# Expert weights stored with an expert's tiles side by side in each row, and loaded two tiles at a time

## The chip, the cores and the metric

The kernel runs on one core of a Trainium2 chip. The metric is the time of one execution on the device, in microseconds (us).

## The reference

The reference runs two transformer blocks over 256 tokens of width 1024, in float32. The first has a mixing sublayer (stick-breaking attention and gated linear attention) and a convolutional FFN. The second has a pooling and attention sublayer and a mixture of 32 experts, of which each token takes 4. Only the experts matter here:

```python
def expert_block(args):
    xblk, e = args
    gu = xblk @ w_gate_up[e] + b_gate_up[e]           # w_gate_up[e]: 1024 x 2048
    gate = jnp.minimum(gu[:, :D_EXPERT], SWIGLU_LIMIT)
    up = jnp.clip(gu[:, D_EXPERT:], -SWIGLU_LIMIT, SWIGLU_LIMIT)
    act = gate * jax.nn.sigmoid(SWIGLU_ALPHA * gate) * (up + 1)
    return act @ w_down[e] + b_down[e]                # w_down[e]: 1024 x 1024
```

Each expert brings 12.6 million bytes of weights that are used once, so the 32 experts read 403 MB from DRAM.

## The kernel before

The first block, the second block's attention and the router come first; then the experts run in order, 0 to 31 (the expert with the most tokens is exchanged with number 16 on the way, so SP reads from a table on the chip which expert's weights to load).

An expert's weights are six tiles of 128 partitions by 4096 floats (16 KB in each partition, 2048 KB in all, called 2 MB below): tiles 0 and 1 hold the gate matrix, 2 and 3 the up matrix, 4 and 5 the down matrix. Here a tile is numbered through all experts: tile 6e + j is tile j of expert e, so tile 100 is the first down tile of expert 16. In DRAM (`wexp`) the array is [32, 6, 128, 4096]: each tile is one contiguous piece.

Tiles go through a ring of 11 slots (`RING`), made of pools `ra`, `rb`, `rx`, `rc`, `re` and `rd`. `ring_tile` takes the next slot; `eload` issues the load on SP's DMA queue. SP runs its loads in program order. A load waits until PE has made its last use of the tile that held the slot before, and each of the 8 semaphores for loads (`DMAHW0` to `DMAHW7`) must have counted its previous load, so at most 8 loads are under way.

PE runs one expert in this order: `hidden` multiplies the gate tiles (32 matmuls into `g`, 16 for each tile), then the up tiles (32 into `u`), both at L1398; `turn` transposes; `down` (L1423) multiplies the two down tiles, 16 for each tile. For expert 16, `over_hidden` and `over_down` run the tokens beyond 64 through the same six tiles once more, so PE keeps these tiles for a second sweep, and the down tiles are used last of all by the ordinary `down`. Experts 30 and 31 are written out by hand at the end, with the last two down tiles loaded in smaller pieces.

```python
def eload(i, t=None, cuts=(0, 4096)):
    if t is None:
        t = ring_tile()
    src = a["wexp"][i // 6, i % 6]
    ...
    for p, q in zip(cuts, cuts[1:]):
        nc.sync.dma_start(out=t[:, p:q], in_=src[:, p:q])
    return t
```

Of the kernel before, what the change touches and what calls it, by code (L numbers as in the profile page):

```python
# [8 lines left out]
F32 = mybir.dt.float32  # L9
# [10 lines left out]
P = 128  # L20
# [4 lines left out]
NE = 32  # L25
# [3 lines left out]
RING_A = 3  # L29
RING_B = 2  # L30
RING_X = 2
RING_C = 4
RING = RING_A + RING_B + RING_X + RING_C
HOT = 16
HOT_FROM = 4
HOT_TO = 30
# [83 lines left out]
def layout(inp):  # L120
    a = {k: np.asarray(v) for k, v in inp.items()}
    o = {}
    o["xT"] = a["x"][0].T.reshape(DC, P, T).transpose(1, 0, 2)
    col = lambda v: np.asarray(v).reshape(-1, P).T
    vec = np.zeros((P, NVEC), np.float32)
    for name, v in (("norm_mix", a["norm_mix_g"]), ("b_gate", a["b_gate"]), ("gla_norm", a["gla_norm_g"]),
                    ("norm_ffn", a["norm_ffn_g"]), ("conv_w", a["conv_w"]), ("conv_b", a["conv_b"]),
                    ("norm_final", a["norm_final_g"]), ("attn_norm", a["g_attn_norm_2"]),
                    ("b_pool", a["b_pool_2"]), ("pool_scale", a["pool_scale_2"]), ("q_a", a["g_q_a_2"]),
                    ("kv_a", a["g_kv_a_2"]), ("out_pool", a["g_out_pool_2"]), ("out_attn", a["g_out_attn_2"])):  # L130
        s, e = VEC[name]
        vec[:, s:e] = col(v)
    o["vecs"] = vec
    o["cst"], o["cst1"], o["cst2"] = constants()
    w = a["w_in"][0]
    kp = lambda m: m.reshape(-1, P, m.shape[-1]).transpose(1, 0, 2)
    o["wga"] = kp(w[:, 3072:3088])
    o["win"] = np.stack([kp(w[:, s:s + 512]) for _, s in W_IN_ORDER])
    o["wau"] = a["w_alpha_up"][0]
    o["bal"] = a["b_alpha"]  # L140
    o["wbr"] = np.stack([kp(a["w_branch_sb"][0]), kp(a["w_branch_gla"][0])])
    o["wout"] = np.stack([kp(a["w_out"][0][:, s:s + 512]) for s in (0, 512)])
    wf = a["w_ffn_in"][0]
    o["wfi"] = np.stack([kp(np.concatenate([wf[:, b:b + 128] for b in
                                            (256 * j, 2816 + 256 * j, 256 * j + 128, 2944 + 256 * j)], 1))
                         for j in range(11)])
    o["wfo"] = kp(a["w_ffn_out"][0])
    w2 = a["w_in_2"][0]
    kr = w2[:, 896:928]
    o["win2"] = np.stack([kp(np.concatenate([w2[:, 512:896]] + [kr, kr[:, 16:], kr[:, :16]] * 2, 1)), kp(w2[:, :512])])  # L150
    wq = a["w_q_b_2"][0].reshape(256, 8, 96)
    o["wq"] = kp(np.concatenate([wq, wq[:, :, 80:96], wq[:, :, 64:80]], 2).reshape(256, 1024))
    wkv = a["w_kv_b_2"][0].reshape(128, 8, 128)
    o["wkv"] = np.concatenate([wkv[:, :, :64].reshape(128, 512), wkv[:, :, 64:].reshape(128, 512)], 1)
    o["wpool"] = a["w_pool_2"][0].transpose(1, 0, 2)
    o["pos"] = a["positions_2"]
    o["wo2"] = kp(a["w_out_2"][0])
    o["gf2"] = np.concatenate([col(a["g_ffn_norm_2"]), col(a["g_final_2"])], 1)
    o["wr"] = kp(a["w_router_2"][0])
    o["br"] = a["b_router_2"]  # L160
    wgu = a["w_gate_up_2"][0].reshape(NE, 2, 4, P, 2, D)
    wdn = a["w_down_2"][0].reshape(NE, 1, 2, 4, P, D)
    o["wexp"] = np.concatenate([wgu.transpose(0, 4, 1, 3, 2, 5).reshape(NE, 4, P, 4096),
                                wdn.transpose(0, 1, 2, 4, 3, 5).reshape(NE, 2, P, 4096)], 1)
    o["wexp"][NE - 1, 4:6] = wdn[NE - 1, 0].reshape(2, 4, P, 2, 512).transpose(3, 2, 0, 1, 4).reshape(2, P, 4096)
    o["bgu"] = np.concatenate([a["b_gate_up_2"][0].reshape(NE, 2, 2, 512).transpose(2, 0, 1, 3).reshape(64, 1024)] * 2, 0)
    o["bdn"] = a["b_down_2"][0]
    return {k: np.ascontiguousarray(v) for k, v in o.items()}


def build(nc, tc, a, out, dump=lambda name, ap: None, upto=99):
# [6 lines left out]
    with ctx:  # L178
        enter = ctx.enter_context
        enter(tc.manual_schedule(engines={PE, mybir.EngineType.SP}))  # L180
        cp = enter(tc.tile_pool(name="cp", bufs=1))
        ring = [enter(tc.tile_pool(name="ra", bufs=RING_A))] * RING_A
        rx = enter(tc.tile_pool(name="rx", bufs=RING_X))
        aux = enter(tc.tile_pool(name="aux", bufs=4, space=PSUM))
        front = ExitStack()
        fenter = front.enter_context
# [31 lines left out]
        who, who_at = {}, []  # L218

        def eload(i, t=None, cuts=(0, 4096)):  # L220
            if t is None:
                t = ring_tile()
            src = a["wexp"][i // 6, i % 6]
            if HOT_FROM <= i // 6 <= HOT_TO:
                if i // 6 not in who:
                    who.clear()
                    who[i // 6] = nc.values_load(who_at[0][0:1, i // 6:i // 6 + 1], engines=[mybir.EngineType.SP],
                                                 min_val=0, max_val=NE - 1)
                src = a["wexp"][bass.ds(who[i // 6], 1), i % 6].rearrange("o p n -> (o p) n")
            for p, q in zip(cuts, cuts[1:]):  # L230
                nc.sync.dma_start(out=t[:, p:q], in_=src[:, p:q])
            return t

        def bank(pool, name):
            return pool.tile([P, 512], F32, name=name)
# [233 lines left out]
        for tt in range(2):  # L469
            o = aps[:, tt * 256:(tt + 1) * 256]  # L470
# [80 lines left out]
        for par in range(2):  # L551
            rows = slice(par * 64, par * 64 + 64)
            for hh in range(2):
                h = 2 * hh + par
                for tt in range(2):
                    o = og[par][:, hh * 256 + tt * 128:hh * 256 + (tt + 1) * 128]
                    mm(o, gv[:, tt, h * 128:(h + 1) * 128], attT[:, par, hh * 2 + tt, :],
                       start=hh == 0 and tt == 0, stop=False, skip_group_check=True)
                for n in range(1, 4):
                    o = og[par][:, hh * 256 + n * 64:hh * 256 + (n + 1) * 64]  # L560
# [204 lines left out]


        ats.close()
        ring.extend([enter(tc.tile_pool(name="rb", side="left", bufs=RING_B))] * RING_B)
        tp = xs.enter_context(tc.tile_pool(name="fp", side="right", bufs=2))
        table("gelu_apprx_tanh_and_others")  # L770
        acc = [bank(aux, "aux") for _ in range(4)]
# [37 lines left out]
        for j in range(11):  # L809
            w = wload(a["wfi"][j].rearrange("p k n -> p (k n)")) if j else wf0  # L810
            if j % 2 == 1 or j == 10:
                k0 = 4 * (j // 2)
                n = min(4, NF - k0)
# [36 lines left out]
        for c2 in range(4):  # L850
            q = tp.tile([P, 2, 2, T], F32, name="nsq", bufs=2)
# [58 lines left out]
        wexp = [eload(i) for i in range(RING - RING_C - 2)]  # L910
# [18 lines left out]
        ra = rb = b3.tile([P, 2, T], F32, name="pt")  # L929
# [140 lines left out]
        prs_done = [False]  # L1070
# [43 lines left out]
        for step, _ in enumerate(hd):  # L1114
            if step == 1:
                next(pm_)
                next(res)
            if step == 3:
                next(res)
            if prs_done[0] and len(wexp) < RING - RING_C - 1:  # L1120
                bx.close()
                ring[:0] = [enter(tc.tile_pool(name="rc", side="left", bufs=1))]
                wexp.append(eload(len(wexp)))
            if step >= 14:
                fill(outp, 1)
        b3x.close()
        ring[:0] = [enter(tc.tile_pool(name="re", side="left", bufs=1))]
        wexp.append(eload(len(wexp)))
        fill(outp, 99)
        wexp.append(eload(len(wexp)))  # L1130
        x2m = bX.tile([P, 2, D], F32, name="X")
# [26 lines left out]
        front.close()  # L1158


        ring[:0] = [enter(tc.tile_pool(name="rd", side="left", bufs=RING_C - 2))] * (RING_C - 2)
        mo = enter(tc.tile_pool(name="mo", side="right", bufs=1))
        rt = ExitStack()
        rp = rt.enter_context(tc.tile_pool(name="rp", side="right", bufs=1))
# [19 lines left out]
        for tt in range(2):  # L1184
            for nh in range(2):
# [4 lines left out]
                o = hT[:, tt, 4 * nh:4 * nh + 4, :].rearrange("p a b -> p (a b)")  # L1190
# [7 lines left out]
        for tt in range(2):  # L1198
            for c in range(DC):
                q = 32 * (c % 4)  # L1200
# [265 lines left out]
        def over_rest(e, wx, room, block):  # L1466
            with over_if(e, block):
                def fetch(j):
                    for i in range(2):
                        nc.scalar.dma_start(out=wx[i], in_=a["wexp"][e, j + i])  # L1470

                fetch(0)
                over_hidden(e, wx, wx, room, block, own=True, between=lambda: fetch(2))
                fetch(4)
                over_down(e, wx, room, block, own=True)
# [15 lines left out]

        LAST = 6 * NE - 8
        for e in range(NE - 2):
            while len(wexp) < 6 * e + 6:
                wexp.append(eload(len(wexp)))
            wg, wu, wd = (wexp[6 * e + 2 * i:6 * e + 2 * i + 2] for i in range(3))
            odd = e % 2
            um = wk.tile([P, 512], F32, name="um")
# [5 lines left out]
                scatter(onehots([0, 1], gcol, "og"), ot)  # L1504
                at = turn(um)
            if odd:
                while len(wexp) < min(6 * e + 4 + RING, LAST):
                    wexp.append(eload(len(wexp)))
            if e and not odd:
                combine(*pend, 0)  # L1510
                at = turn(um)
# [7 lines left out]
            elif odd:  # L1519
# [3 lines left out]
                gather(xg, oh, 2 * CAP, 1)  # L1523
                ot_next = ot_tile()
                scatter(onehots([e + 1, e + 2], gcol, "og"), ot_next)
            while len(wexp) < min(6 * e + 4 + RING, LAST):
                wexp.append(eload(len(wexp)))
            if not odd:
                ds = rooms["ds"]
            ps = down(at, wd)  # L1530
# [9 lines left out]
                           start=False, stop=False, skip_group_check=True)  # L1540
            for dh in range(2):
                nc.scalar.copy(ds[odd * 64:odd * 64 + 64, dh * 512:(dh + 1) * 512], ps[dh * 64:dh * 64 + 64, :])  # L1542
            while len(wexp) < min(6 * e + 6 + RING, LAST):
                wexp.append(eload(len(wexp)))
            if odd:
                pend = (ot, ds)
                ot = ot_next
# [2 lines left out]
        p, q = NE - 2, NE - 1  # L1550
# [58 lines left out]
        wx = [ring_tile() for _ in range(2)]  # L1609
# [24 lines left out]
```

## Time and profile before

| | |
|---|---|
| median of 3 runs | 1415.34 us (1415.24 to 1419.24) |
| the profiled execution's own time | 1415.02 us |
| its span, first to last instruction | 1413.2 us |
| PE busy | 1364.8 us, 97% of the span |
| DVE, ACT, POOL busy | 33%, 25%, 11% of the span |
| loads of expert tiles on SP's queue | 190 of 2 MB and 6 smaller ones |

The span lies 1.8 us under the execution's own time; what lies around it is start and end. Times in the trace count from the start of the span. PE is TensorE, SP the engine that issues the loads; a load "lands" when its semaphore has its full count.

### The profile page before, as it was taken

To read this page: it belongs to the slowest core of one execution; us is meant where nothing else is said; L and a number is where in the kernel's file an instruction comes from. 1 tells how busy PE (TensorE), PEld (TensorE's weight loads), DVE (VectorE), ACT (ScalarE), POOL (GpSimd) and SP (SyncE) were. 2 spreads that over 40 slices of the span, in tenths; PEclk is the share of its full clock that TensorE was granted. 3 is DMA by queue.
4 is the path that set the end of the run, shared out by engine and by line. 5 is a ranking of instruction groups with operands and counts; after the bars stand their busy time and mean duration, and the time that the engine had idled before them with its cause. 6 is when DMAs were issued, how large, how long until landed. Compare 5 with 4: busy or idle time off the path is not lost.

```text
span 1413.2 us, 18906 instructions
## 1 busy us (share of the span) xinstructions
PE 1364.8 (97%) x7842; PEld 791.8 (56%) x7842; DVE 472.9 (33%) x777; ACT 354.7 (25%) x583; POOL 151.6 (11%) x240
## 2 busy tenths in 40 slices
PE   8999999999999999999999999998999999999896
PEld 7999999999997733433333333343334334333333
DVE  5556778676698521101101111110111111111111
ACT  5355755444455510010001001000100100100002
POOL 0001221112120021011011011010101101101010
PEclk9999999999999999999999999999999999999999
DMA  8334257345356789999999999999999999999995
GB/s 301 150 142 155 98 229 289 129 179 209 148 203 258 312 372 429 419 428 428 428 427 428 429 427 427 428 428 427 428 428 427 428 429 426 427 429 427 428 427 219
DMA packets 38866, 482.13 MB, mean 341 GB/s; under 512 B 4289, under 2 KB 8018, under 8 KB 9586
## 3 DMA queue, kind: packets, MB, share of 16 engines
q1 hardware_dynamic: 38722, 480.69, 81.8%
q8 instruction: 64, 1.05, 0.3%
q14 instruction: 32, 0.26, 0.0%
q10 hardware_dynamic: 48, 0.13, 0.0%
HBM read 479.75 MB, written 1.05 MB: 340 GB/s over the span
## 4 chain that ended last, share of the span: by engine, by line
PE 73%; DMA 19%; DVE 4%; ACT 2%; issue 1%; POOL 1%; SPq 0%; ACTq 0%; POOLq 0%
DMA w<-in_wexp 19%; PE tr L1423 12%; PE g L1398 12%; PE u L1398 11%; PE mm L306 6%; PE mm L307 6%; PE mm L309 6%; PE tr L1369 3%; PE aux L1479 3%; PE mm L348 2%; PE aux L1098 1%; PE aux L804 1%; PE aux L803 1%; PE aux L805 1%; DMA w<-in_win 1%; PE u L1393 1%
## 5 line engine op out<-in xcount | busy, mean ns | idle before, releaser
L1398 PE MATMUL u<-w,X 128*64 128x512 f32 x1056 | 235.4, 596 | 6.5 <-DMA w<-in_wexp 6.5
L1398 PE MATMUL g<-w,X 128*64 128x512 f32 x1056 | 234.3, 595 | 1.6 <-DMA w<-in_wexp 0.8
L1423 PE MATMUL tr<-w,sg 128*64 128x512 f32 x992 | 223.1, 603 | 9.1 <-ACT ot L1379 6.9
L1403 DVE TENSOR_SCALAR um<-g 128x512 f32<-128x512 f32 x32 | 22.1, 692 | 503.8 <-PE g L1398 503.8
L1398 PEld LDWEIGHTS u<-w,X 128*64 128x64 f32 x1056 | 72.3, 137 | 148.7 <-issue 135.6
L1423 PEld LDWEIGHTS tr<-w,sg 128*64 128x64 f32 x992 | 69.3, 138 | 149.7 <-issue 136.0
L1398 PEld LDWEIGHTS g<-w,X 128*64 128x64 f32 x1056 | 72.7, 137 | 141.5 <-issue 138.2
L306 PE MATMUL mm<-w,hi 128*128 128x256 f32 x608 | 150.4, 286 | 0.0
L307 PE MATMUL mm<-w,hi 128*128 128x256 f32 x608 | 148.0, 281 | 0.0
L300 DVE TENSOR_TENSOR lo<-w,hi 128x1024 fp32r<-128x1024 f32 x108 | 132.4, 1226 | 36.3 <-ACT hi L299 36.3
L299 ACT ACTIVATE hi<-w 128x1024 fp32r<-128x1024 f32 x108 | 114.0, 1060 | 90.6 <-PE mm L307 72.1
L306 PEld LDWEIGHTS mm<-w,hi 128*128 128x128 f32 x608 | 115.1, 189 | 1.4 <-issue 0.9
L307 PEld LDWEIGHTS mm<-w,hi 128*128 128x128 f32 x608 | 115.3, 190 | 0.4 <-issue 0.2
L1542 ACT COPY X<-tr 64x512 f32<-64x512 f32 x60 | 34.8, 580 | 225.0 <-PE tr L1423 221.3
L309 PE MATMUL mm<-w,lo 128*128 128x256 f32 x608 | 84.6, 281 | 0.0
L1407 DVE TENSOR_SCALAR sg<-u 128x512 f32<-128x512 f32 x33 | 22.8, 691 | 182.1 <-PE u L1398 182.1
L1416 ACT COPY sg<-tr 128x512 f32<-128x512 f32 x33 | 19.4, 587 | 256.0 <-PE tr L1413 256.0
L309 PEld LDWEIGHTS mm<-w,lo 128*128 128x128 f32 x608 | 77.4, 188 | 0.0
L1404 ACT ACTIVATE sg<-um 128x512 f32<-128x512 f32 x32 | 20.2, 630 | 220.7 <-DVE um L1403 220.7
L1383 POOL CAST pick<-selb 128x128 fp32r<-128x128 f32 x32 | 9.3, 293 | 573.3 <-PE u L1393 573.3
L1479 PE MATMUL aux<-X,ot 128*128 128x512 f32 x128 | 61.6, 606 | 0.0
L1369 PE MATMUL tr<-oh,xh 128*128 128x128 f32 (+1 forms) x256 | 51.3, 282 | 4.8 <-DVE X L1372 4.8
(477 smaller groups left out, 1690.5 us busy)
## 6 DMA issues: line engine op xcount, KB each, us to landing
w<-in_wexp SPq DMA_DIRECT2D x190, 2048.0 KB, 29.1
w<-in_win SPq DMA_DIRECT2D x11, 2048.0 KB, 7.4
w<-in_wfi SPq DMA_DIRECT2D x11, 2048.0 KB, 9.0
w<-in_wfo SPq DMA_DIRECT2D x5, 2048.0 KB, 13.3
w<-in_wbr SPq DMA_DIRECT2D x2, 2048.0 KB, 8.7
w<-in_wout SPq DMA_DIRECT2D x2, 2048.0 KB, 7.3
w<-in_wo SPq DMA_DIRECT2D x2, 2048.0 KB, 7.7
w<-in_wexp SPq DMA_DIRECT2D x3, 1024.0 KB, 34.3
```

The lines of the kernel that those rows point to most:

```text
L299: act(hv, src, AF.Copy)
L300: vtt(lv, src, hv.bitcast(F32), op=OP.subtract)
L306: mm(ps, hv[:, k, :], xh[:, k, :], start=start and k == 0, stop=False, skip_group_check=True)
L307: mm(ps, hv[:, k, :], xl[:, k, :], start=False, stop=False, skip_group_check=True)
L309: mm(ps, lv[:, k, :], xh[:, k, :], start=False, stop=k == nk - 1, skip_group_check=True)
L348: mm(ps[tt], lhs, (hv, hv, lv)[part][:, kk, :], start=u == 0 and part == 0 and kk == 0, stop=u == 3 and part == 2 and kk == 1)
L1369: mm(ps[:, j * n:(j + 1) * n], xn[i // 2][:, i % 2, c * 128:(c + 1) * 128], oh[:, i % 2, :], start=i == 0, stop=i == 3)
L1398: mm(gu[i][hf * 64:hf * 64 + 64, :], xg[:, k, :], ws[k // 4][:, (k % 4) * D + hf * 512:(k % 4) * D + (hf + 1) * 512], start=late and k == ...
L1407: vts(t, gu[1], LIMIT, -LIMIT, op0=OP.min, op1=OP.max)
L1423: mm(ps[dh * 64:dh * 64 + 64, :], at[:, k % 4, k // 4, :], wd[k // 4][:, (k % 4) * D + dh * 512:(k % 4) * D + (dh + 1) * 512], start=k == ...
L1479: mm(y[tt][dh], ot[rows, tt * 128:(tt + 1) * 128], ds[rows, dh * 512:(dh + 1) * 512], start=False, stop=False, skip_group_check=True)
L1542: nc.scalar.copy(ds[odd * 64:odd * 64 + 64, dh * 512:(dh + 1) * 512], ps[dh * 64:dh * 64 + 64, :])
```

## The change

In DRAM the six tiles of an expert now lie side by side in each row: `wexp` is [32, 128, 24576], so one partition's part of a tile is 16 KB out of a row of 96 KB, and the parts of tiles j and j+1 follow each other.

The ring keeps its 11 slots, but its parts are now windows of 3 (`ra`), 2 (`rb`), 2 (`rx`), 2 (`rc`, in place of `rc` and `re`) and 2 (`rd`) slots, in which tiles of one or of two slots follow each other and wrap to the start.

From tile 22 on, `eload_to` takes two tiles at once where both are of one expert, where the next two slots are of one part and where at least 8 tiles remain. Such a pair is one 4 MB transfer with runs of 32 KB in each partition, has one semaphore, and its two slots come free together.

```diff
+    o["wexp"] = o["wexp"].transpose(0, 2, 1, 3).reshape(NE, P, 6 * 4096)
...
+        def slots(name, n, **kw):
+            return enter(tc.tile_pool(name=name, bufs=1, side="left", **kw)).ring(n * 4096 * 4, name=name)
+
+        ring = [slots("ra", RING_A)] * RING_A
+        rx = slots("rx", RING_X)
...
             for p, q in zip(cuts, cuts[1:]):
-                nc.sync.dma_start(out=t[:, p:q], in_=src[:, p:q])
+                nc.sync.dma_start(out=t[:, p:q], in_=src[:, o + p:o + q])
             return t
+
+        def eload_to(wexp, limit):
+            while len(wexp) < limit:
+                i = len(wexp)
+                if i >= 2 * RING and i % 6 != 5 and ring[0] is ring[1] and i + 2 <= 6 * NE - 8:
+                    if i + 2 > limit:
+                        break
+                    ring.extend([ring.pop(0), ring.pop(0)])
+                    t = ring[-1].tile([P, 8192], F32, name="w")
+                    eload(i, t, (0, 8192))
+                    wexp += [t[:, 0:4096], t[:, 4096:8192]]
+                else:
+                    wexp.append(eload(i))
...
-            if prs_done[0] and len(wexp) < RING - RING_C - 1:
+            if prs_done[0]:
                 bx.close()
-                ring[:0] = [enter(tc.tile_pool(name="rc", side="left", bufs=1))]
-                wexp.append(eload(len(wexp)))
...
-        ring[:0] = [enter(tc.tile_pool(name="re", side="left", bufs=1))]
-        wexp.append(eload(len(wexp)))
+        ring[:0] = [slots("rc", 2, reuse_waits="tile")] * 2
+        eload_to(wexp, len(wexp) + 2)
...
-            while len(wexp) < min(6 * e + 4 + RING, LAST):
-                wexp.append(eload(len(wexp)))
+            eload_to(wexp, min(6 * e + 4 + RING, LAST))
```

SP's order shows the pairs in two places. The first is the loads after expert 16's: a name `w_n` is one ring tile, 128x4096 is 2 MB and 128x8192 is 4 MB, and the rows between that only set addresses are left out. Before, these are tiles 107 to 113, one load each:

```order
L231 DMA w_7687<-in_wexp 128x4096 [waits DMAHW2_49,PE_49]
L231 DMA w_7689<-in_wexp 128x4096 [waits DMAHW3_49,PE_49]
L231 DMA w_7701<-in_wexp 128x4096 [waits DMAHW4_49,PE_49]
L231 DMA w_7703<-in_wexp 128x4096 [waits DMAHW5_49,PE_49]
L231 DMA w_7724<-in_wexp 128x4096 [waits DMAHW6_49,PE_49]
L231 DMA w_7726<-in_wexp 128x4096 [waits DMAHW7_49,PE_49]
L231 DMA w_7779<-in_wexp 128x4096 [waits DMAHW0_49,PE_49]
```

After the change the rows of the same place hold the pairs (104, 105), (106, 107), (108, 109), (110, 111) and (112, 113), and the single tile 114:

```order
L236 DMA w_7435<-in_wexp 128x8192 [waits DMAHW0_49,PE_49]
L236 DMA w_7621<-in_wexp 128x8192 [waits DMAHW2_49,DMAHW1_49,PE_49]
L236 DMA w_7623<-in_wexp 128x8192 [waits DMAHW3_49,PE_49]
L236 DMA w_7654<-in_wexp 128x8192 [waits DMAHW4_49,PE_49]
L236 DMA w_7707<-in_wexp 128x8192 [waits DMAHW6_49,DMAHW5_49,PE_49]
L236 DMA w_7709<-in_wexp 128x4096
```

Tile 110 had a load and a wait of its own, and now waits with tile 111. The pair (110, 111) takes the two slots of the pair (99, 100); the pair (112, 113) takes the slot of tile 101 and one of the pair (102, 103).

The second place is the last tiles that pairs can take. Before, these are the loads of tiles 179 to 184:

```order
L231 DMA w_9145<-in_wexp 128x4096 [waits DMAHW2_49,PE_49]
L231 DMA w_9147<-in_wexp 128x4096 [waits DMAHW3_49,PE_49]
L231 DMA w_9159<-in_wexp 128x4096 [waits DMAHW4_49,PE_49]
L231 DMA w_9161<-in_wexp 128x4096 [waits DMAHW5_49,PE_49]
L231 DMA w_9182<-in_wexp 128x4096 [waits DMAHW6_49,PE_49]
L231 DMA w_9307<-in_wexp 128x4096 [waits DMAHW7_49,PE_49]
```

After the change the rows are the pair (178, 179), tile 180, the pair (181, 182), tile 183 and tile 184:

```order
L236 DMA w_9021<-in_wexp 128x8192 [waits DMAHW6_49,DMAHW5_49,PE_49]
L236 DMA w_9023<-in_wexp 128x4096
L236 DMA w_9035<-in_wexp 128x8192 [waits DMAHW7_49,PE_49]
L236 DMA w_9056<-in_wexp 128x4096 [waits DMAHW0_49,PE_49]
L236 DMA w_9181<-in_wexp 128x4096
```

The last pair joins expert 30's second gate tile (181) to its first up tile (182); what follows is loaded singly, as before. Over the whole of SP's order 64 loads are 128x8192, 31 of them up to the pair (99, 100) and 35 up to (108, 109). Up to tile 21 the rows are those of before, and the rows of PE are the same throughout.

## Rows read from the trace of the kernel before

**Rows 1.** The page: span, and DMA share and rate in 40 slices of 35.3 us.
```profile
span 1413.2 us, 18906 instructions
...
DMA  8334257345356789999999999999999999999995
...
GB/s 301 150 142 155 98 229 289 129 179 209 148 203 258 312 372 429 419 428 428 428 427 428 429 427 427 428 428 427 428 428 427 428 429 426 427 429 427 428 427 219
```

**Rows 2.** Busy time by engine in one stretch of two experts (53.4 us).
```profile
core 0: us, PE busy (x) PEld busy (x) DVE busy (x) ACT busy (x) POOL busy (x), PEclk, DMA share, GB/s
...
1046.89:1100.29 53.40, 52.62 (x247) 20.07 (x247) 6.92 (x10) 5.14 (x10) 4.50 (x10) 1.00 1.01 428
```

**Rows 3.** PE's waits for expert tiles, whole span: us in total, times, longest.
```profile
PE u L1398 <- DMA w<-in_wexp: 6.5, 9, 1.2
...
PE g L1398 <- DMA w<-in_wexp: 0.8, 1, 0.8
...
PE tr L1432 <- DMA w<-in_wexp: 0.4, 1, 0.4
```

**Rows 4.** PE in order of time, experts 15 and 16: start, length, instruction, [idle before].
```profile
914.42 3.65 PE L1398 MATMUL u<-w,X 128*64 128x512 f32 x16 [0.30 <-DMA w<-in_wexp]
...
938.89 3.65 PE L1398 MATMUL u<-w,X 128*64 128x512 f32 x16 [0.43 <-DMA w<-in_wexp]
...
943.79 3.65 PE L1398 MATMUL u<-w,X 128*64 128x512 f32 x16 [1.25 <-DMA w<-in_wexp]
...
986.05 7.09 PE L1423 MATMUL tr<-w,sg 128*64 128x512 f32 x32 [0.73 <-ACT sg L1416]
```

**Rows 5.** PE in order of time, experts 30 and 31 (same columns).
```profile
1345.14 7.09 PE L1398 MATMUL g<-w,X 128*64 128x512 f32 x32
...
1353.07 3.65 PE L1398 MATMUL u<-w,X 128*64 128x512 f32 x16 [0.41 <-DMA w<-in_wexp]
...
1357.97 3.65 PE L1398 MATMUL u<-w,X 128*64 128x512 f32 x16 [1.25 <-DMA w<-in_wexp]
...
1377.56 3.65 PE L1398 MATMUL u<-w,X 128*64 128x512 f32 x16 [0.59 <-DMA w<-in_wexp]
...
1394.87 3.46 PE L1432 MATMUL tr<-w,sg 128*64 128x256 f32 x30 [0.40 <-DMA w<-in_wexp]
```

**Rows 6.** SP's issues of tiles 100, 110, 111, 114 and 182: start, length.
```profile
909.60 0.33 SPq L231 DMA_DIRECT2D w<-in_wexp  x1
...
970.36 0.33 SPq L231 DMA_DIRECT2D w<-in_wexp  x1
...
989.75 0.33 SPq L231 DMA_DIRECT2D w<-in_wexp  x1
...
1000.63 0.33 SPq L231 DMA_DIRECT2D w<-in_wexp  x1
...
1314.17 0.34 SPq L231 DMA_DIRECT2D w<-in_wexp  x1
```

**Rows 7.** Issue to landing, us, of tiles 8, 100, 110 and 182.
```profile
w<-in_wexp SPq DMA_DIRECT2D x1, 2048.0 KB, 7.6
...
w<-in_wexp SPq DMA_DIRECT2D x1, 2048.0 KB, 39.0
...
w<-in_wexp SPq DMA_DIRECT2D x1, 2048.0 KB, 28.8
...
w<-in_wexp SPq DMA_DIRECT2D x1, 2048.0 KB, 38.9
```

**Rows 8.** SP's queue at 620 to 730 and 417 to 418.2 us: packets, MB, share.
```profile
q1 hardware_dynamic: 3222, 46.91, 100.3%
...
q1 hardware_dynamic: 233, 0.47, 100.7%
```

**Rows 9.** A w_ffn_out tile issued at 322.18; all engines' window while it moves.
```profile
w<-in_wfo SPq DMA_DIRECT2D x1, 2048.0 KB, 13.5
...
331.20:335.20 4.00, 4.00 (x36) 4.00 (x35) 2.92 (x5) 1.23 (x2) 0.86 (x1) 1.00 1.01 434
```

More of the change, by code (lines that the diff above doesn't have):

```diff
@@ L181, in build @@
         cp = enter(tc.tile_pool(name="cp", bufs=1))
-        ring = [enter(tc.tile_pool(name="ra", bufs=RING_A))] * RING_A
-        rx = enter(tc.tile_pool(name="rx", bufs=RING_X))
+        def slots(name, n, **kw):
+            return enter(tc.tile_pool(name=name, bufs=1, side="left", **kw)).ring(n * 4096 * 4, name=name)
+        ring = [slots("ra", RING_A)] * RING_A
+        rx = slots("rx", RING_X)
         aux = enter(tc.tile_pool(name="aux", bufs=4, space=PSUM))
@@ L220, in eload @@
         def eload(i, t=None, cuts=(0, 4096)):
+            e, o = i // 6, i % 6 * 4096
             if t is None:
                 t = ring_tile()
-            src = a["wexp"][i // 6, i % 6]
-            if HOT_FROM <= i // 6 <= HOT_TO:
-                if i // 6 not in who:
+            src = a["wexp"][e]
+            if HOT_FROM <= e <= HOT_TO:
+                if e not in who:
                     who.clear()
-                    who[i // 6] = nc.values_load(who_at[0][0:1, i // 6:i // 6 + 1], engines=[mybir.EngineType.SP],
-                                                 min_val=0, max_val=NE - 1)
-                src = a["wexp"][bass.ds(who[i // 6], 1), i % 6].rearrange("o p n -> (o p) n")
+                    who[e] = nc.values_load(who_at[0][0:1, e:e + 1], engines=[mybir.EngineType.SP],
+                                            min_val=0, max_val=NE - 1)
+                src = a["wexp"][bass.ds(who[e], 1)].rearrange("o p n -> (o p) n")
             for p, q in zip(cuts, cuts[1:]):
-                nc.sync.dma_start(out=t[:, p:q], in_=src[:, p:q])
+                nc.sync.dma_start(out=t[:, p:q], in_=src[:, o + p:o + q])
             return t
+        def eload_to(wexp, limit):
[10 more added lines that the diff above has]
+                    wexp.append(eload(i))
         def bank(pool, name):
@@ L767, in build @@
         ats.close()
-        ring.extend([enter(tc.tile_pool(name="rb", side="left", bufs=RING_B))] * RING_B)
+        ring.extend([slots("rb", RING_B)] * RING_B)
         tp = xs.enter_context(tc.tile_pool(name="fp", side="right", bufs=2))
@@ L1158, in build @@
         front.close()
-        ring[:0] = [enter(tc.tile_pool(name="rd", side="left", bufs=RING_C - 2))] * (RING_C - 2)
+        ring[:0] = [slots("rd", RING_C - 2, reuse_waits="tile")] * (RING_C - 2)
         mo = enter(tc.tile_pool(name="mo", side="right", bufs=1))
@@ L1469, in fetch @@
                     for i in range(2):
-                        nc.scalar.dma_start(out=wx[i], in_=a["wexp"][e, j + i])
+                        nc.scalar.dma_start(out=wx[i], in_=a["wexp"][e, :, (j + i) * 4096:(j + i + 1) * 4096])
                 fetch(0)
@@ L1493, in build @@
         for e in range(NE - 2):
-            while len(wexp) < 6 * e + 6:
-                wexp.append(eload(len(wexp)))
+            eload_to(wexp, 6 * e + 6)
             wg, wu, wd = (wexp[6 * e + 2 * i:6 * e + 2 * i + 2] for i in range(3))
@@ L1506, in build @@
             if odd:
-                while len(wexp) < min(6 * e + 4 + RING, LAST):
-                    wexp.append(eload(len(wexp)))
+                eload_to(wexp, min(6 * e + 4 + RING, LAST))
             if e and not odd:
@@ L1525, in build @@
                 scatter(onehots([e + 1, e + 2], gcol, "og"), ot_next)
-            while len(wexp) < min(6 * e + 4 + RING, LAST):
-                wexp.append(eload(len(wexp)))
+            eload_to(wexp, min(6 * e + 4 + RING, LAST))
             if not odd:
@@ L1542, in build @@
                 nc.scalar.copy(ds[odd * 64:odd * 64 + 64, dh * 512:(dh + 1) * 512], ps[dh * 64:dh * 64 + 64, :])
-            while len(wexp) < min(6 * e + 6 + RING, LAST):
-                wexp.append(eload(len(wexp)))
+            eload_to(wexp, min(6 * e + 6 + RING, LAST))
             if odd:
```

## The prediction

> **What bounds the kernel now.** I read the page first. From the sixteenth slice on, about 530 us, the DMA engines are busy nine tenths or more and move 426 to 429 GB/s to the end [rows 1]: the expert tiles arrive as one stream without a gap, and the stream could be the bound. The second view is busy time over two experts: they last 53.40 us, and PE is busy for 52.62 of it [rows 2]. Their twelve tiles are 25.2 MB, which at 428 GB/s takes 58.8 us. So PE is faster than the stream by 2.7 us an expert, yet it hardly waits: the third view gives all its waits for expert tiles as 6.5 + 0.8 + 0.4 = 7.7 us [rows 3]. The two fit together because PE starts with a full ring of eleven tiles, 54 us of stream, and eats it up. The fourth view, PE in order of time, shows where. It catches the stream at tiles 93, 98 and 99 (0.30, 0.43 and 1.25 us, 1.98 in all) [rows 4]. Then expert 16's second sweep gives the stream time to draw ahead, and PE catches it again at the end, down to 0.40 us before the last piece [rows 5].
>
> So the end is set by both. PE's own work would end at 1413.2 - 7.7 = 1405.5 us, and what is added is the lateness of the stream at the worst place: the largest difference, over all tiles, between its landing and the moment at which a PE that had never waited would have asked for it. Before, this largest difference is 7.7 us. For the changed kernel I need two things: how far the stream moves, and how much later a tile counts as landed because it belongs to a pair.
>
> **What a pair saves.** A 2 MB tile gives each of the 16 DMA engines 8 packets of 16 KB and a small one for the semaphore. If a 32 KB run is one packet, a pair has 9 packets per engine in place of 18. The price of a packet apart from its bytes comes from two stretches of SP's queue: 110 us with 3222 packets and 46.91 MB, busy 100.3% of 16 engines, which is 1765 us; and 1.2 us with 233 small packets and 0.47 MB, 100.7%, which is 19.3 us [rows 8]. With a per packet and b per MB, 3222a + 46.91b = 1765 and 233a + 0.47b = 19.3 give b = 37.1 us and a = 8.2 ns. A pair then saves 9 x 8.2 = 74 ns of its 9.8 us. No row shows a 32 KB packet, so this is bounded on both sides: if the run is moved as two packets, only the semaphore's is saved, 8 ns; if everything but the bytes vanished, 18 x 8.2 = 148 ns. I take 74, since a is a price of the packet and the sizes in the two stretches differ by a factor of several without upsetting it. The 64 pairs save 4.7 us, of which 2.3 us by tile 100 (31 pairs) and 2.6 us by tile 109 (35 pairs).
>
> The row shows more on size. A load issued to an idle queue lands after 7.6 us, the stream spends 4.9 us on a tile (2.1 MB at 428 GB/s), so 2.7 us of a load are lead, and in the stream this lead is hidden behind the loads under way [rows 1, 7]. The Trainium skill (SBUF — State Buffer, The DMA setup-cost knee) has it that every transfer pays about 2 us that do not scale with its bytes, and advises the largest single transfer. By that rule 64 transfers fewer would save 128 us, by the row none of the 2.7 us, as long as the queue is never empty.
>
> **What a pair costs.** First, neither of its tiles can be read before both have landed. The worst place is the pair (181, 182). Tile 182 landed at 1314.17 + 38.9 = 1353.1 [rows 6, 7]. PE reads tile 181 in the second half of the sweep that begins at 1345.14, so at 1348.7; it had by then waited all but the last 0.41 + 1.25 + 0.59 + 0.40 = 2.65 of its 7.7 us, so without waits at 1343.6 [rows 3, 5]. The difference is 9.5 us where the largest was 7.7: 1.8 us more, if the stream is where it was. After this pair the tiles are single and their differences stay those of before.
>
> Second, a pair's two slots come free together, and this matters once. Before expert 16's second sweep is over, PE lets go of tile 99 at 970.36 (tile 110 is issued), of tile 100 only at 989.75, in the `down` that starts at 986.05 [rows 4, 6]. The pair (110, 111) needs both. By then PE is also later than before: the pair (99, 100) lands when 100 did, 909.60 + 39.0 = 948.6, less 2.3 saved, 946.3; a PE without waits would ask for tile 99 at 943.79 - 1.98 = 941.8; it has waited 4.5 us in place of 2.0 [rows 4, 6, 7]. So the pair is issued at 989.75 + 2.5 = 992.3, and with its lead of 2.7 us its bytes flow from 995.0. The stream's last work before it, tile 109, ended one tile ahead of tile 110, 970.36 + 28.8 - 4.9 = 994.3, less 2.6 saved, 991.7 [rows 6, 7]. The DMA engines are idle for 3.3 us. The next pair (112, 113) needs tile 103's slot, which was free at 1000.63: 1000.63 + 2.5 + 2.7 = 1005.8, while (110, 111) is done at 995.0 + 9.7 = 1004.7; another 1.1 us [rows 6]. Elsewhere the queue is about 6 to 8 tiles deep (28.8 to 39.0 us from issue to landing at 4.9 each [rows 7]), and a pair's wait for its second slot, 3.5 us of PE's work [rows 4], is hidden by it.
>
> Costed at nothing: the order of the first 22 tiles and PE's program, which do not change; SP's issue time, 0.33 us a load [rows 6], under a queue of that depth; and the 96 KB row pitch of the single tiles, beside which a tile of `w_ffn_out` stands: it lies in rows of 88 KB and moved at 434 GB/s, no slower than the contiguous expert tiles [rows 9].
>
> **The sum.** The stream moves by 3.3 + 1.1 - 4.7 = -0.3 us, the worst place adds 1.8: +1.5 us. The profiled execution took 1415.02 us, so 1416.5; the median of the runs shown is 0.3 us above it, 1415.34, and against that I forecast 1416.8 us. With 8 ns a pair, PE is 4.6 us late at tile 100, the idle times are 3.1 and 1.1, the pairs save 0.5, and the sum is 1.8 + 4.2 - 0.5 = +5.5 us. With 148 ns, PE is 0.2 us late, the idle times are 3.6 and 1.1, the pairs save 9.5, and it is 1.8 + 4.7 - 9.5 = -3.0 us. About 0.3%, 4.2 us, is what a measurement of this kernel can tell from no change.
>
> **The rivals.** *The 32 KB run is no single packet*, so a transfer of twice the size saves nothing and the pair's lag and the idle at tile 110 stay: +5.5 us, 1420.8, slower. It decides from a saving under 28 ns a pair on (each ns moves the sum by 60 ns). For it: no row has a packet above 16 KB. Against it: every 16 KB run of the trace is one packet, 46.91 MB in 3222 packets, a ninth of them semaphores [rows 8].
>
> *The row pitch slows all tiles.* Each 1% on the 162 tiles from 22 to 183 is 162 x 49 ns = 7.9 us on a stream that sets the end; it decides from 0.35% on, and 0.5% gives some 1420.8 us. Against it stands the 88 KB pitch [rows 9]; for it, that 96 KB is three times a power of two and 88 is not. The Trainium skill (DMA: Bandwidth & Descriptors, Latency and other measured facts) tells of copies at a pitch of 512 KiB that ran at 207 GB/s where a padded pitch had 214, and worse beyond; an estimate by that page's 3% would be 24 us, 1441. The trace has no such pitch.
>
> *The engines never run dry and more is saved.* Without the 4.4 us of idle the sum is 1.8 - 4.7 = -2.9 us, 1412.4; with 148 ns as well, 1.8 - 9.5 = -7.7 us, 1407.6, and PE's own work and the pair's lag allow little more. Faster by 0.3% needs 95 ns a pair without idle, or 170 with it, which is past the bound. The skill's 2 us per transfer would also end here, at PE's limit of about 1407; the hidden lead [rows 7] speaks against it.
>
> **Chances.** The forecast, within about 3 us: 64 in 100. No single packet: 12, of which 9 are past 0.3%. Pitch: 10, of which 8. No idle or more saved: 12, of which 6. Setup cost saved: 2. Of the forecast's own 64, 6 fall past +0.3%, for an idle time longer than counted. Faster 0.08, same 0.69, slower 0.23. The range of 8 in 10 runs from the lower bound of the saving, 1412, to the upper one, 1421.5.
>
> **What would show it.** In the trace after: SP's queue with about 74 ns less per pair, packets of 32 KB and 430 to 431 GB/s between 700 and 900 us; a dent in the DMA row near 990 to 1005 us; waits of PE of some 2 to 3 us at first tiles of pairs near 915 and 940 and in the last four experts, about 9 us in all, where the second half of expert 30's gate sweep waits. The prediction is wrong if the rate stays at 428 (the first rival), if it falls below (the second), or if there is no dent.

## The result

The changed kernel is slower. Against the kernel before on the same chip its ratio is 1.0051 (95% interval 1.0036 to 1.0065): 1424.26 us in the median of 7 executions, where the kernel before had 1415.83. The medians lie 8.4 us apart; the ratio, by which the runs below are compared too, is 7.2 us. The times of the changed kernel spread from 1418.5 to 1426.5 us and go with the mean granted clock of PE: 0.992 goes with 1418.5, 0.986 with 1426.5. The profiled execution is the quickest of them (1418.5 us), so the profile shows the least of what happens. The forecast was 1416.8 us, in a range of 1412 to 1421.5.

The page of the changed kernel, cut to the lines of [rows 1]:

```profile
span 1416.7 us, 18611 instructions
...
DMA  8334265444456789999999999999999999999995
GB/s 305 148 143 158 81 238 238 179 179 179 191 200 267 307 367 430 420 427 431 430 428 432 431 426 434 425 435 389 376 434 432 423 434 430 429 429 433 430 424 222
```

The stream is faster: the ten slices from 600 to 950 us have 425 to 435 GB/s, 430 in the mean, where they had 427 to 429; but two slices near 1000 us have 389 and 376. SP's queue from 700 to 900 us (packets, MB, share of 16 engines), of the kernel before:

```profile
q1 hardware_dynamic: 5858, 85.33, 100.4%
```

and of the changed kernel:

```profile
q1 hardware_dynamic: 3604, 85.87, 100.1%
```

A 32 KB run is one packet: 2254 packets fewer are 16 pairs (nine packets less on each of 16 engines), and they moved 0.54 MB more in the same time, 1.27 us of stream, 79 ns for each pair (74 were forecast).

The dent that was forecast is there. Busy time of the changed kernel in four stretches (the last two columns are the share of the DMA engines and their rate):

```profile
core 0: us, PE busy (x) PEld busy (x) DVE busy (x) ACT busy (x) POOL busy (x), PEclk, DMA share, GB/s
...
984.00:988.00 4.00, 3.31 (x18) 1.10 (x16) 0.00 (x0) 0.59 (x1) 0.00 (x0) 1.00 0.84 360
988.00:992.00 4.00, 3.27 (x20) 1.13 (x18) 0.00 (x0) 0.59 (x1) 0.00 (x0) 1.00 0.23 94
992.00:996.00 4.00, 4.00 (x22) 1.41 (x20) 0.00 (x0) 0.00 (x0) 0.00 (x0) 1.00 0.43 131
996.00:1000.00 4.00, 4.00 (x20) 1.25 (x17) 0.00 (x0) 1.16 (x2) 0.00 (x0) 1.00 0.91 393
```

The engines are idle for (0.16 + 0.77 + 0.57 + 0.09) x 4 = 6.4 us here, where 3.3 were forecast; for the other 1.1 us of the forecast the shares from 1004 to 1016 us are 0.90, 0.93 and 0.93, so 1.0 us. Together that is 7.4 in place of 4.4. The pair (110, 111) was to be issued at 992.3; SP's issue came at 993.9, 4.2 us after tile 111's in [rows 6], because PE was later than the 2.5 us of the prediction (1.7 us of the difference; where the rest comes from stays open):

```profile
993.90 11.22 SPq L236 DMA_DIRECT2D w<-in_wexp  x2
```

Why PE was later is seen in PE's order of time (start, length, instruction, [idle before]) and its waits. The matmuls that use the down biases, in the kernel before:

```profile
576.89 3.70 PE L1539 MATMUL aux<-X,um 32*128 32x512 f32 x8 [0.45 <-ACT um L1536]
```

The same matmuls and three sweeps of the changed kernel:

```profile
577.52 3.67 PE L1552 MATMUL aux<-X,um 32*128 32x512 f32 x8 [1.26 <-DMA X<-in_bdn]
...
581.66 8.61 PE L1414 MATMUL g<-w,X 128*64 128x512 f32 x32
...
918.71 5.35 PE L1414 MATMUL u<-w,X 128*64 128x512 f32 x16 [2.33 <-DMA w<-in_wexp]
...
1331.02 8.78 PE L1414 MATMUL u<-w,X 128*64 128x512 f32 x32 [2.20 <-DMA w<-in_wexp]
```

Three things stand here that the kernel before did not have. PE waits 1.26 us for `X<-in_bdn`, the 128 KB of down biases that ACT's queue loads once, in expert 2. Its waits for expert tiles are fewer and longer: 7.4 us in 5 waits, 2.33 us at the most, where [rows 3] have 7.7 us in 11 and 1.25 at the most. And behind each of these three waits a sweep takes longer than its like: 8.61 and 8.78 us where 32 matmuls take 7.09 [rows 5], 5.35 us where 16 take 3.65. The granted clock says why: it is at 1.2 in place of 2.4 GHz for a time. Each such fall costs 1.5 to 1.7 us. The profile has five falls before the last 10 us; two of them, near 817 and 960 us, stand behind none of these waits, and the kernel before has two as well (near 708 and 974 us). Two of the stretches:

```profile
916.00:924.00 8.00, 5.67 (x19) 1.48 (x17) 0.00 (x0) 0.00 (x0) 0.00 (x0) 0.79 0.99 422
...
1332.00:1336.00 4.00, 4.00 (x14) 1.19 (x12) 0.00 (x0) 0.00 (x0) 0.00 (x0) 0.57 1.02 436
```

### The profile page after: what moved, and what is told of

It is laid out like the page before. It is cut to its first block, busy times and chain, and to the rows that moved or that the text cites. A ratio compares the mean times of both kernels' runs of the same rounds, so it can differ in the third digit from the quotient of the medians.

```text
span 1416.7 us, 18611 instructions
## 1 busy us (share of the span) xinstructions
PE 1368.5 (97%) x7842; PEld 793.0 (56%) x7842; DVE 473.6 (33%) x777; ACT 354.6 (25%) x583; POOL 151.3 (11%) x240
## 4 chain that ended last, share of the span: by engine, by line
PE 83%; DMA 10%; DVE 4%; ACT 2%; issue 1%; POOL 1%; SPq 0%; ACTq 0%; POOLq 0%
PE u L1414 15%; PE tr L1439 14%; PE g L1414 14%; DMA w<-in_wexp 8%; PE mm L324 6%; PE mm L325 6%; PE mm L327 6%; PE tr L1385 4%; PE aux L1495 3%; PE mm L366 2%; PE aux L1116 1%; PE aux L822 1%; PE aux L821 1%; PE aux L823 1%; PE u L1409 1%; DVE X L1388 1%
## 5 line engine op out<-in xcount | busy, mean ns | idle before, releaser
L1414 PE MATMUL g<-w,X 128*64 128x512 f32 x1056 | 237.3, 602 | 1.6 <-DMA w<-in_wexp 0.8
```

What stands on the lines that cost most here:

```text
L1414: mm(gu[i][hf * 64:hf * 64 + 64, :], xg[:, k, :], ws[k // 4][:, (k % 4) * D + hf * 512:(k % 4) * D + (hf + 1) * 512], start=late and k == ...
```

## The experiments

Each kernel was timed in five rounds against the kernel before on the same chip. Most differ from the changed kernel only in the condition under which two tiles are taken as a pair:

```diff
-                if i >= 2 * RING and i % 6 != 5 and ring[0] is ring[1] and i + 2 <= 6 * NE - 8:
+                if <tiles> and i % 6 != 5 and ring[0] is ring[1]:
```

**again**: the changed kernel, unaltered.

> The changed kernel once more, for a second profile. It is 7 us slower in the median but only 3.5 us in its first profile, whose mean granted clock is 0.992; in the other executions the clock is 0.986 to 0.991 and the time follows it. Theory A (long waits): where PE stands still for about 2 us at the first tile of a pair, the granted clock falls behind it to about 0.5 for some 3.4 us, 1.7 us lost each time; the two kernels differ because a pair makes waits of 2.2 to 2.3 us out of several of 0.3 to 1.25 us. A expects here 1420 to 1426 us, at least five stretches with a fallen clock where the kernel before has two, and most of the added ones directly behind a wait of PE of over 1.5 us. Theory B (the 32 KB transfers themselves, by what else they hold up): as many falls, but away from PE's waits for expert tiles, and waits for other loads beside them.

Measured: 1422.54 us, ratio 1.0047 (1.0034 to 1.006). The bias load was late again (a wait of 1.49 us), and PE's clock was low behind it for longer: the mean over 576 to 592 us is 0.68. But the waits of 2.28 and 2.19 us for expert tiles, which are the places of theory A, have no fall behind them this time, and the profile has three stretches with a fallen clock before the end, not five or more. The wait for the biases is a wait for another load, as theory B named it.

**single**: the layout and the ring of the change, no pairs.

```diff
+                if False:
```

> The new layout and ring, but every tile loaded singly. Theory A: the row pitch costs nothing, the queue moves 426 to 428 GB/s between 620 and 950 us, PE waits as before (0.3 to 1.3 us, 7 to 8 us in all), the clock is that of before and the ratio to before 0.998 to 1.002. Rival (pitch): under 425 GB/s, and at 0.5% less rate a ratio of 1.003 or more.

Measured: 1415.95 us, ratio 1.0001 (0.9992 to 1.001), 140.78 MB from 620 to 950 us as before. PE's waits for expert tiles are 5.5 us in all, a little under the 7 to 8 that were expected. The row pitch of 96 KB costs nothing.

**two**: a pair's slots, filled by two transfers.

```diff
-                    eload(i, t, (0, 8192))
+                    eload(i, t, (0, 4096, 8192))
```

> The pairs keep their two slots, which come free together, but each is loaded by two transfers of 2 MB, so that the first tile can be read when it has landed. Theory A: no wait of PE over 1.5 us for an expert tile, no more than two or three stretches with a fallen clock; no packet is saved and the queue is idle for 3 to 5 us near 990 to 1005 us, so 1417 to 1420 us, a ratio of 1.001 to 1.0035. Theory C (the joint release of two slots does it all): 1422 us or more, with the clock as low as in the changed kernel. Theory B: as A here, so A and B are told apart by the other runs.

Measured: 1418.36 us, ratio 1.0013 (1.0004 to 1.0021), no wait of PE for an expert tile over 1.24 us, and a share of 0.78 from 992 to 996 us: with what lacks up to 1008 us the queue is idle for some 1.3 us, less than the 3 to 5 that were expected. The biases land after 6.8 us, though the slots beside them are those of pairs, and from 584 to 624 us the queue is never idle. The joint release alone is a smaller part of the loss, as A had it and C had not.

**clear**: `<tiles>` is `(22 <= i < 88 or 114 <= i < 158)`.

> Pairs of 4 MB only where PE is well behind the stream: among tiles 22 to 87 and 114 to 157, 43 pairs; single tiles where PE catches the stream and where expert 16's slots are awaited. Theory A: 43 x 74 ns = 3.2 us of the stream saved, no idle queue, no wait of PE over 1.3 us, the clock that of before: 1411.5 to 1413.5 us, a ratio of 0.997 to 0.999. Theory B: the clock falls as often in proportion to the pairs, 1418 us or more.

Measured: 1418.01 us, ratio 1.0005 (0.9996 to 1.0014), times from 1414.1 to 1420.2. Theory A's range is missed. The median just meets the bound of theory B, 1418 us, but the kernel before has a median of 1416.45 us on this chip, and the ratio shows no loss. The profile has no idle queue at 990 us and no wait over 1.25 us for a tile, but one of 1.99 us for the bias load, and the queue is at 69 and 74% from 612 to 620 us. So what A names is not where this kernel loses; that made theory D.

**apart** and **early**: the same places without the first pairs, and the first pairs without the rest. `<tiles>` is `(46 <= i < 88 or 114 <= i < 158)` and `22 <= i < 46`.

> Pairs only among tiles 46 to 87 and 114 to 157 (33 pairs), so that none is in flight while the ring is full and the 128 KB load of the down biases is under way, none where PE catches the stream, none at expert 16's slots. Theory D (tolerance): what pairs take away is the ring's tolerance for a PE that is late; where the queue is only two or three tiles deep (500 to 620 us) a pair that waits for its second slot lets the queue run dry as soon as PE is late, and PE is made late there because the bias load lands 1.7 to 2.4 us later beside 4 MB transfers. D expects no wait for the bias load, it lands after 6.7 us, no idle queue, 33 x 74 ns = 2.4 us saved: 1413 to 1415 us, a ratio of 0.9975 to 0.999, and a time that hardly follows the clock. Theory A (long waits at the pairs where PE meets the stream) and theory B (pairs as such lower the clock): A expects what the pairs away from the meeting places gave, a ratio of about 1.000; B a clock of 0.990 or less and 1417 us or more.

> Pairs only among tiles 22 to 45 (10 pairs), where the ring is full; all later tiles single. Theory D: the bias load lands after 8 to 9 us, PE waits 1 to 2 us for it, the queue is idle for 1 to 4 us between 590 and 620 us, and the time is 1417 to 1420 us, a ratio of 1.001 to 1.003, higher where the clock is low. Theory A: the waits at the later meeting places are single ones again, so the time is that of before less 10 x 74 ns: a ratio of 0.999 to 1.000.

Measured: apart 1413.23 us, ratio 0.9983 (0.9974 to 0.9992), the quickest kernel of the study; the biases land after 6.6 us and PE does not wait for them; ten of eleven executions lie between 1412.97 and 1414.4 us at clocks of 0.991 to 0.994. early 1419.54 us, ratio 1.0028 (1.0019 to 1.0037). Ten pairs cost 4.0 us where they should have saved 0.7. The load of the biases from issue to landing, in the kernel before:

```profile
X<-in_bdn ACTq DMA_DIRECT2D x1, 128.0 KB, 6.7
```

and in early:

```profile
X<-in_bdn ACTq DMA_DIRECT2D x1, 128.0 KB, 8.8
```

What follows in early is in its windows: the clock is at half for a while, then, some 25 us later, the queue has nothing to move:

```profile
584.00:588.00 4.00, 4.00 (x8) 1.16 (x8) 0.00 (x0) 1.16 (x2) 0.00 (x0) 0.50 1.03 442
...
612.00:616.00 4.00, 4.00 (x21) 1.19 (x17) 0.00 (x0) 0.00 (x0) 0.27 (x1) 1.00 0.63 270
616.00:620.00 4.00, 4.00 (x19) 1.45 (x21) 0.00 (x0) 1.16 (x2) 0.00 (x0) 1.00 0.79 270
```

The same 612 to 616 us in apart:

```profile
612.00:616.00 4.00, 4.00 (x22) 1.34 (x20) 0.00 (x0) 0.00 (x0) 0.00 (x0) 1.00 1.02 434
```

**before4** and **after4**: more matmuls ahead of expert 3, so that PE is later, in the kernel before and in the changed one.

```diff
-                    mm(gu[i], pick, bgu[:, i, :], start=True, stop=False, skip_group_check=True)
+                    for _ in range(10 if e == 3 and i == 0 else 1):
+                        mm(gu[i], pick, bgu[:, i, :], start=True, stop=False, skip_group_check=True)
```

> The kernel before with nine more bias matmuls in a row ahead of expert 3's gate matmuls (the same product again; the result stays), so that PE is some 4 us later there with no wait and at a full clock. Theory D: the ring of single tiles tolerates it; PE's later waits for tiles get shorter by as much, the queue is not idle, and the time is within 0.5 us of before. A rival (every us of PE is paid, the stream's bound is not reached): 4 us more, a ratio of 1.0027.

> The changed kernel with the same nine matmuls more ahead of expert 3. Theory D: here the queue runs dry between 590 and 620 us, every tile from there on is later by 3 to 4 us, and of the added 4 us at least 2.5 are paid: 1425 to 1429 us. Theory A (only the later meeting places matter, and there a later PE waits less): the time of the changed kernel, 1422 to 1424.5 us, or less.

Measured: before4 ratio 1.0006 (0.9997 to 1.0015), after4 1.0051 (1.0037 to 1.0064). The matmuls were shorter than I had thought: the row of before4 has 2.60 us for ten, 2.1 us more than for one.

```profile
583.07 2.60 PE L1394 MATMUL g<-bgu,pick 128*128 128x512 f32 x10
```

The kernel before tolerates them. In the changed kernel 2.1 us would be 0.0015, which is within the intervals: this pair of runs says nothing on D.

**mid**, **from46** and **nohot**: `<tiles>` is `27 <= i < 46`; `i >= 46 and i + 2 <= 6 * NE - 8`; and `(46 <= i < 88 or i >= 114) and i + 2 <= 6 * NE - 8`.

> Pairs only among tiles 27 to 45 (8 pairs): the ring is as full as where the pairs of 22 to 45 stood, but no pair moves while the 128 KB bias load is under way. Theory D1 (the late bias load starts it: PE waits, its clock falls, and it is the late PE that lets the queue run dry): the load lands after 6.7 us, PE does not wait for it, no idle queue, a ratio of 0.999 to 1.0005. Theory D2 (the joint release of two slots is enough, with or without the bias load): an idle queue between 590 and 620 us and a ratio of 1.0015 to 1.003, as with the pairs of 22 to 45.

> The changed kernel without its pairs before tile 46 (54 pairs stay, expert 16's and the last ones among them). If the early pairs cost some 4 us (early: 1.0028 with 0.7 us saved), this is some 4 us faster than the changed kernel: 1417 to 1419.5 us, a ratio of 1.001 to 1.0025, with the queue idle for 4 to 7 us near 990 to 1005 us. If the meeting places and expert 16 carry the loss (theory A), it stays at 1421 us or more.

> As the run with pairs from tile 46 on, but single tiles from 88 to 113 too: the pairs at expert 16's slots are gone, the last ones stay (43 pairs). If the idle queue at expert 16's slots is the other part, it is gone: 43 x 74 ns = 3.2 us saved against 1.8 us for the lag of the last pair, 1413 to 1415.5 us, a ratio of 0.998 to 1.0. If the pairs at the end carry the rest (PE's waits of 2.2 us in experts 28 to 30), 1416.5 us or more.

Measured: mid 1416.51 us, ratio 1.0005 (0.9996 to 1.0014), bias load 6.7 us, no wait for it. Its queue is not quite full all the time: the share is 0.90 from 592 to 596 us and 0.79 from 612 to 616, with a clock of 0.51 from 584 to 588. from46 1419.27 us, 1.0025 (1.0016 to 1.0034), with the queue idle for 8.2 us in 988 to 1000 us, where 4 to 7 were expected:

```profile
988.00:992.00 4.00, 3.31 (x16) 0.98 (x12) 0.00 (x0) 0.58 (x1) 0.00 (x0) 1.00 0.42 180
992.00:996.00 4.00, 3.27 (x18) 1.33 (x18) 0.00 (x0) 0.59 (x1) 0.00 (x0) 1.00 0.01 4
996.00:1000.00 4.00, 4.00 (x22) 1.29 (x18) 0.00 (x0) 0.00 (x0) 0.00 (x0) 1.00 0.53 164
```

nohot 1415.48 us, 0.9999 (0.9989 to 1.001), at the upper end of its first expectation, with no idle queue there, and with a wait near the end that costs clock:

```profile
1327.32 8.68 PE L1414 MATMUL u<-w,X 128*64 128x512 f32 x32 [2.19 <-DMA w<-in_wexp]
```

**only22**, **before6** and **mid6**: pairs at (22, 23) and (24, 25) alone (`22 <= i < 27`); and 27 in place of 10 in the loop above, in the kernel before and in mid.

> Pairs only at (22, 23) and (24, 25), the two that move while the bias load is under way; all other tiles single. Theory D1 (the late bias load and the clock that falls behind it are the cost): the load lands after 8 to 9 us, PE waits 1.2 to 2 us for it and loses up to 5 us of clock behind it, and a ring of single tiles doesn't make that good: a ratio of 1.002 to 1.0035. Theory D3 (the load makes PE late, but only with the pairs of 27 to 45 does a late PE stop the stream): PE as late, the queue not idle, a ratio of 0.9995 to 1.001.

> The kernel before with 26 more bias matmuls in a row ahead of expert 3 (the same product again; the result stays); nine of them made PE 2.1 us later, so these some 6 us. D1 (a PE that is 6 us late there stops the stream, whatever the tiles): the queue is idle near 612 us, a ratio of 1.0015 to 1.003. D3 (single tiles tolerate it): 1.000 to 1.001.

> The run with pairs at 27 to 45 with the same 26 matmuls. D1: as much as in the kernel before with these matmuls, a ratio of 1.0015 to 1.003. D3: clearly more than there, 1.002 to 1.0035 against 1.000 to 1.001.

Measured: only22 1420.25 us, ratio 1.0026 (1.0015 to 1.0037): two pairs out of 64 cost as much as all ten of early, which is in D1's range and not in D3's. Its bias load took 8.7 us:

```profile
X<-in_bdn ACTq DMA_DIRECT2D x1, 128.0 KB, 8.7
```

Its executions with a clock of 0.994 took 1416.0 to 1417.6 us, those of 0.988 to 0.992 took 1418.7 to 1422.4; the profiled one is of the first kind, so no trace shows how the slower ones lost their time. before6 1418.96 us, 1.0019 (1.0009 to 1.0028); mid6 1423.28 us, 1.0045 (1.0032 to 1.0058). The 26 matmuls are some 6 us of PE at 2.4 GHz; in the profile of before6 the 27 take 8.68 us, since the clock falls in them. They cost 2.7 us in a ring of single tiles and 5.7 us (0.0040, uncertain by 0.0016) in one with eight pairs. In mid6 the queue runs dry in two stretches:

```profile
592.00:596.00 4.00, 4.00 (x20) 1.55 (x20) 0.00 (x0) 0.00 (x0) 0.00 (x0) 1.00 0.33 139
596.00:600.00 4.00, 4.00 (x19) 1.19 (x15) 0.05 (x1) 0.00 (x0) 0.00 (x0) 1.00 0.64 225
616.00:620.00 4.00, 4.00 (x19) 1.19 (x15) 0.00 (x0) 0.15 (x1) 0.09 (x1) 1.00 0.61 262
```

and in before6 in the first of them alone:

```profile
596.00:600.00 4.00, 4.00 (x20) 1.29 (x18) 0.00 (x0) 0.00 (x0) 0.00 (x0) 1.00 0.54 127
```

D1 is right that a late PE stops the stream there whatever the tiles; D3 is right that pairs make it dearer, about twofold, though the difference of 3.0 us is itself uncertain by some 2.6.

## Why the prediction was wrong

The runs split the change by where the pairs stand. The forecast column takes its terms from the prediction (74 ns a pair, 4.4 us of idle, 1.8 us of lag); a ratio of 0.001 is 1.4 us, and a difference of two ratios is uncertain by some 2 us.

| pairs among tiles | count | forecast, us | measured, us | from |
|---|---|---|---|---|
| 22 to 45 | 10 | -0.7 | +4.0, +3.1 | early; again less from46 |
| 46 to 87 and 114 to 157 | 33 | -2.4 | -2.4 | apart |
| 88 to 113 | 11 | +3.6 | +3.7 | from46 less nohot |
| 158 to 182 | 10 | +1.1 | +2.3 | nohot less apart |
| all | 64 | +1.6 | +6.7, +7.2 | again; the result |

**The step that failed** is the list of costs. It had no load but SP's own: the 128 KB of biases on ACT's queue, PE's wait for them and the clock behind it were put at nothing without a reason. And the costs of a pair closed with the sentence "Elsewhere the queue is about 6 to 8 tiles deep (28.8 to 39.0 us from issue to landing at 4.9 each [rows 7]), and a pair's wait for its second slot, 3.5 us of PE's work [rows 4], is hidden by it." The loads behind it are tiles 100, 110 and 182. Where the first ten pairs stand the ring is full and the stream hangs on PE's releases: in the kernel before tile 21 was issued at 546.7 us and landed 12.7 us later, tile 26 took 19.8 us, tile 33 14.6 and tile 44 24.1, where a lone load takes 7.6. So the queue is one to three and a half tiles deep there beyond a tile's own transfer. That alone is not the loss (mid, 1.0005), but there is little depth to hide a late PE (before6). The row to see it in was on the page: "426 to 429 GB/s to the end" passes over the slice from 565 to 601 us, which has 419 [rows 1]. That is where the biases' load shares the engines with the stream, in the kernel before:

```profile
572.00:576.00 4.00, 4.00 (x20) 1.15 (x16) 0.00 (x0) 0.00 (x0) 0.00 (x0) 1.00 1.01 360
```

Of the 5.1 to 5.6 us between the columns, 3.8 to 4.7 belong to the first row of the table.

**What happens in their place**, as the runs show it. The bias load is the start. It lands after 6.6 to 7.2 us in the ten profiles without a 4 MB transfer beside it and after 8.4 to 9.2 us in the six with one. The Trainium skill (DMA: Bandwidth & Descriptors, Queues, rings and completion order) states that a DMA engine goes round the queues that have work for it, one packet at a time. For a packet the Trainium skill gives some 9 to 17 descriptors (orders to move one piece of data) as typical. The trace agrees with the going round, but its turns are of one run each: the biases are 32 rows of 4 KB and 16 semaphores, and in the changed kernel 16 of these rows start from 572.70 to 574.37 us together with 16 runs of 32 KB, in apart 16 of them from 575.42 to 576.34 with 16 runs of 16 KB. An engine thus moves one run of the stream, then one row of the biases. A 16 KB run of the stream holds an engine for 0.61 us, one of 32 KB for twice that, and the biases are two rows and a semaphore for each engine, so three turns: an estimate of 1.8 us more. In the kernel before the biases landed at 575.9, 1.0 us before PE's use of them; now PE waits 1.3 to 2.0 us. Then comes the clock. In all six profiles with this wait it falls to 1.2 GHz for a time before 592 us (mean over 576 to 592 us: 0.89 twice, 0.68 four times), in four of the ten without it (0.79), in six not at all. Over 16 us a mean of 0.89 costs 1.8 us and one of 0.68 costs 5.1. So PE is later by some 2.6 us (the result's profile) to 6.2 us (again) where the ring is full, an estimate from the wait, less the 0.45 us that stood there before, and the clock. The queue then runs dry (early, near 594 and 616 us), and the stream never makes up for it: in early tile 99 lands at 948.8 us and tile 182 at 1358.1, in the kernel before at 943.7 and 1353.0, 5.1 us earlier both times. Pairs on that stretch make it dearer (mid6 against before6), but without the late load they cost nothing that can be measured (mid).

That the wait causes the fall is not settled by this: there are falls without it. Nor did any run move the load of the biases away from the pairs, or keep the clock up. What is shown is that two pairs beside the load cost 3.7 us and eight pairs after it 0.7 us or nothing, and that with two transfers in the slots of the pairs (two) the load is in time.

**Right, with its size.** A pair saves 79 ns in the trace (74) and 33 pairs gave the 2.4 us that were summed for them. The first rival, no single packet, is out, and so is the second: single, 1.0001, leaves the pitch no cost. Fewer transfers saved nothing beyond the packets, so the lead of 2.7 us was indeed hidden. Expert 16's pairs stop the queue as worked out; in the trace of the changed kernel for 7.4 us in place of 4.4, with PE 4.2 us late in place of 2.5. That their row of the table comes out at 3.7 us for 3.6 is therefore in part luck: in the profile of from46 the queue is idle for 8.2 us there, and less than that is paid.

**Half right: the end.** The worst place was to be the pair (181, 182). In the second profile it is: PE's last wait is 0.80 us, at 1359.3. In the first, PE's last wait is that for (176, 177) at 1331.0; the clock falls behind it and PE is never waiting again. The lag had its price in the forecast; the clock behind a long wait had none. Over all 16 profiles 5 of the 9 waits for expert tiles of more than 2.1 us had a lower clock in the 3 us behind them, and none of the some 90 shorter ones.

**Against the list of what would show it.** Right: the packets, the saving, the dent, waits of 1.8 to 2.3 us at first tiles of pairs near 915 us and in the last four experts. Wrong: none near 940 in the first profile, 7.4 us in all and not 9, and nothing in the list looked at the 500 to 620 us in which most was lost.

## What to carry to other kernels

Larger transfers are worth a measured price per packet (here 79 ns for each pair of 2 MB tiles), and only while nobody waits for what shares the queue, the slots or the semaphore with them. Before making a stream's transfers larger, list the small loads of other queues that run beside it and the margin with which each is awaited, and read the queue's depth (issue to landing against a lone load) at every stage, not only where the stream is the bound. Pairs kept away from a full ring, from the places where PE catches the stream and from slots that are held long made this kernel faster than both (0.9983); pairs everywhere made it slower.

## What the hardware showed that was not expected

A 128 KB load on ACT's queue took 1.7 to 2.5 us longer than its 6.7 because another queue's runs went from 16 to 32 KB, and an engine moved one of them between any two of its rows. PE's clock fell from 2.4 to 1.2 GHz behind waits of 2.2 to 3.5 us in 5 of 9 cases, and at the same matmuls of one kernel in one execution and not in the next: from execution to execution the changed kernel's mean clock went from 0.986 to 0.992, and its time by 8 us, with nothing altered. On the chip of the first four runs the kernel before has executions of 0.990 at 1416.3 to 1418.6 us and of 0.996 at 1416.3 and 1416.6: the lower mean clock cost that kernel 2.3 us at the most.
